# Splitting one chunk in five of the softmax probabilities on GpSimd, with GpSimd's weight work in the attention's written order

## The chip, the cores and the metric

The kernel runs on one core of one Trainium2 chip. The metric is the device time in microseconds (us) of one execution. The engines are TensorE (PE, whose weight loads have a row of their own, PEld), VectorE (DVE), ScalarE (ACT), GpSimd (POOL) and SyncE (SP), which issues every DMA of this kernel.

## What is computed

Two layers of a block with four mixers side by side, over 1024 latent rows and 256 context rows of width 1024. In each layer a conditioning vector gives scale, shift and gate (the modulation, `silu(c) @ w_mod`), the normalised rows go through one in-projection, two attention mixers (MLA and GQA, four heads each), a state-space scan and a long convolution run on slices of it, and an out-projection joins them. Cut to what matters here:

```python
def block_attention(q, k, v, scale):
    def attend(qblk):
        s = jnp.einsum('bqhgd,bkhd->bhgqk', qblk, k, preferred_element_type=jnp.float32) * scale
        p = jax.nn.softmax(s, axis=-1).astype(v.dtype)
        return jnp.einsum('bhgqk,bkhd->bqhgd', p, v)
...
for l in range(DEPTH):
    need_ctx = l < DEPTH - 1
    sh_l, sc_l, gt_l = [m[:, None, :] for m in modulation(c, w_mod[l], b_mod[l])]
    h_l = rms_norm(x, g_pre[l]) * (1 + sc_l) + sh_l
    p_l = h_l @ w_in[l]
    a_l, a_c = mla_mixer(...)
    g_l, g_c = gqa_mixer(...)
    out_l = jnp.concatenate([a_l, g_l, s_l, y_l], axis=-1) @ w_out[l]
    x = x + gt_l * rms_norm(out_l, g_post[l])
```

Latent queries attend to 1280 keys (1024 latent, 256 context), context queries to the 256 of the context. Context outputs are needed in layer 0 only.

## The kernel before, in words

**Products of two halves.** Most fp32 products are made of three fp32r products: an operand x is split into hi, a copy that rounds it to the type float32r, and lo = x - hi (`lo`, L248, a subtraction on VectorE unless another engine is named). An SBUF tile of halves is written `...h`/`...l` or `...hi`/`...lo`.

**Attention.** `attention` (L1528 on) runs once a layer: from 737 to 1077 us for layer 0 and from about 1820 to 2077 us for layer 1. A unit is one head and 256 queries. Layer 0 has 40 units (two GQA head pairs, then two MLA pairs; in each five blocks of 256 queries, the last of the context; two heads in each), layer 1 has 32. In a unit TensorE makes scores `aS` (latent keys) and `acx` (context keys), VectorE takes their maxima and scales (`am`), ScalarE makes the exponentials `aP` and their sums. The 1280 keys are five chunks of 256, c = 0 to 4. For each chunk TensorE transposes the probabilities into PSUM (`apt`, `tr` at L1651, step T of a chunk), ScalarE copies them to SBUF as float32r (`aPh`, `hi` at L1661, step H), VectorE subtracts (`aPl`, `lo` at L1665, step L), and TensorE multiplies both halves with the values (`apo`, `PV` at L1669, steps Vh and Vl). `apt` shares two PSUM banks (tag `f`) with the modulation products `mps` and the transposes `alb`; `aPh` and `aPl` have three buffers each. The softmax's denominators are summed and inverted on VectorE (`recip`, L1679), spread over 64 columns by GpSimd (`aLB`, `spread` at L1685), transposed (`alb`), and multiplied into the output (`aob`), which is stored.

**The order.** The program is written in the Tile framework; a scheduler places each engine's instructions by a simulated timeline (L1996), except for those that carry one issue-order token: these keep their written order on their engine. `keep` (L193) stamps the token that is set; inside `attention` it is set, and the written order is the table `ORDER` (L1525), which names the steps of a unit and, by +1 or -1, of which neighbouring unit. The DMA loads of keys, values and queries have a token of their own (`fetch`, L1548). The last entry, `X`, is `pump` (L1538), once a unit: it runs the products that the last pump left behind and draws one piece of side work, with the token taken off while it is drawn:

```python
            self.token = None
            more = next(side, self)
            self.token = token
```

**Side work.** `side` (L1934) first splits modulation weights: a piece (`mod_steps`, L325) takes one loaded block `mraw` of 128x1024, copies it to `mhi` and subtracts to `mlo`, both on GpSimd, and leaves four products `mps` and VectorE's addition to `msb` for the next pump. Layer 0 has 24 such pieces (its own gates and layer 1's modulation), layer 1 has 8 (its gates). The finished rows of the gates go out by a store `modg<-msb` (`mod_gates`, L375, the store at L381). Then the pool of these tiles is closed, a pool for the weights of the out-projection is opened in its place (L1941), and 16 pieces (`out_weights`, L1750) each take one loaded block `owr`, copy it to `owh` (L1757) and subtract to `owl`, again on GpSimd. Raw blocks are loaded two (`mraw`) or three (`owr`) pieces ahead by `feed` (L303).

Of the kernel before, what the change touches and what calls it, by code (L numbers as in the profile page):

```python
# [11 lines left out]
F32 = mybir.dt.float32  # L12
# [175 lines left out]
class K:  # L188
# [31 lines left out]
    def f(self, name="f"):  # L220
        return self.psf.tile([128, 512], F32, tag="f", name=name)
# [103 lines left out]
    def mod_steps(self, P, feed, l, blk):  # L325

        ms = P.tile([4, 512], F32, tag="msb", name="msb", bufs=2)
        nc = self.nc
        for k in range(0, 8, 2):
            raw = next(feed)  # L330
            hi, lo = (P.tile([128, 2, 512], F32R, tag="m" + t, name="m" + t, bufs=2) for t in ("hi", "lo"))
            nc.gpsimd.tensor_copy(hi, raw)
            self.lo(lo, raw, hi, nc.gpsimd)

            def products(k=k, hi=hi, lo=lo):
                ps = self.f("mps")
                for j in range(2):
                    self.mm(ps[:4], self.sp[:, k + j], hi[:, j], j == 0, False)
                    self.mm(ps[:2], self.sp[:, k + j, 0:2], lo[:, j], False, j == 1)
                if k == 0:  # L340
                    self.keep(nc.vector.tensor_copy(ms, ps[:4]))
                else:
                    self.tt(ms, ps[:4], ms, ADD)

            self.later.append(products)
            yield ms if k == 6 else None
# [1181 lines left out]
    def attention(self, l, pools, nq, side):  # L1528


        nc = self.nc

        W, L, P = pools
        token = self.token = f"att{l}"
# [3 lines left out]
        def pump():  # L1538

            late, self.later = self.later, []  # L1540
            for f in late:
                f()
            self.token = None
            more = next(side, self)
            self.token = token
            return more is not self or bool(self.later)

        def fetch(dst, src):  # L1548
# [102 lines left out]
        def tr(c, x):  # L1651
            ps = self.f("apt").rearrange("p (k q) -> p k q", k=2)
            for k in range(2):
                for qi in range(2):
                    j = 2 * c + k
                    self.tr(ps[:, k, qi * 128:qi * 128 + 128], x["pt"][qi][:, j * 128:j * 128 + 128])
            hi = W.tile([128, 2, 256], F32R, tag="aPh", name="aPh", bufs=3)
            lo = W.tile([128, 2, 256], F32R, tag="aPl", name="aPl", bufs=3)
            x["P"][c] = (ps, hi, lo)

        def hi(c, x):  # L1661
            ps, h, _ = x["P"][c]
            self.keep(nc.scalar.copy(h, ps))  # L1663

        def lo(c, x):  # L1665
            ps, h, l_ = x["P"][c]
            self.lo(l_, ps, h)

        def PV(c, part, x):  # L1669

# [50 lines left out]
        for c in range(5):  # L1721
            for nm, f in (("T", tr), ("H", hi), ("L", lo)):
                steps[f"{nm}{c}"] = partial(f, c)
            steps[f"Vh{c}"] = partial(PV, c, 1)
            steps[f"Vl{c}"] = partial(PV, c, 2)
        order = []
        for s in self.ORDER.split():
            if s == "X":
                order.append((pump, None, False))
                continue  # L1730
            nm, off = (s[:-2], int(s[-2:])) if s[-2:-1] in ("+", "-") else (s, 0)
            latent = nm[0] in "SM" and nm != "MC" or nm[0] in "THLV" and nm != "LB" and nm[-1] != "4"
            order.append((steps[nm], off, latent))
# [11 lines left out]
        while pump():  # L1745
            pass
# [3 lines left out]
    def out_weights(self, l, P, R):  # L1750
        wh = P.tile([128, 8, 1024], F32R, name="owh")
        wl = P.tile([128, 8, 1024], F32R, name="owl")
        halves = [(k, slice(h, h + 512)) for k in range(8) for h in (0, 512)]
        feed = self.feed(R, "owr", [128, 512], (self.A["w_out"][l, :, k, h] for k, h in halves), 3)
        for k, h in halves:
            raw = next(feed)
            self.nc.gpsimd.tensor_copy(wh[:, k, h], raw)  # L1757
            self.lo(wl[:, k, h], raw, wh[:, k, h], self.nc.gpsimd)
            yield
        self.wo = wh, wl  # L1760
# [239 lines left out]
```

## Time and profile before

| | |
|---|---|
| three runs | 2193.89, 2194.62, 2198.0 us; median 2194.62 |
| the profiled execution | 2194.1 us, span 2192.3 us |
| TensorE busy | 1937.6 us, 88% |
| VectorE busy | 1593.3 us, 73% |
| ScalarE busy | 916.5 us, 42% |
| GpSimd busy | 992.0 us, 45% |
| mean granted clock of TensorE | 0.927 of full |

The profile is of one execution, so its rows are compared with 2194.1 us; 1.8 us of that lie outside the span. Busy shares are means over stages that differ: a change in the attention is read from the attention's rows.

### The profile page before, as it was taken

How to read it: one execution, taken by the hardware profiler on the slowest of the kernel's cores; microseconds unless marked ns; L12 is line 12 of the kernel's file. 1: busy time of each engine (PE TensorE's matmuls, PEld its weight loads, DVE VectorE, ACT ScalarE, POOL GpSimd, SP SyncE). 2: the span in 40 equal slices, each digit the busy share in tenths (PEclk: the TensorE clock that was granted, in tenths of full speed). 3: DMA queues.
4: the chain of work that ended last, by engine and by line, in shares of the span. 5: the costliest groups of instructions: out<-in, count | busy, mean ns of one | idle time of the engine just before them, and what ended most of it. 6: DMA issues, size and time to landing. Idle time of an engine off the chain costs nothing.

```text
span 2192.3 us, 31534 instructions
## 1 busy us (share of the span) xinstructions
PE 1937.6 (88%) x10811; PEld 1617.4 (74%) x10811; DVE 1593.3 (73%) x2982; ACT 916.5 (42%) x1958; POOL 992.0 (45%) x798
## 2 busy tenths in 40 slices
PE   5788998789899899999799998997989949999888
PEld 2577887678778777788577776886767737899866
DVE  8799439855896589789444598389577858999732
ACT  4421233224334467667322322343233317788611
POOL 3757225564661244432155557246675622340034
PEclk7798899899999899999799987998999979999989
DMA  6323365337765546352343423264357673551053
GB/s 222 115 88 119 129 203 142 92 115 212 237 186 183 159 127 180 101 149 69 114 156 113 151 100 144 86 232 145 98 173 221 202 231 100 137 159 54 21 176 131
DMA packets 261249, 316.55 MB, mean 144 GB/s; under 512 B 46655, under 2 KB 203583, under 8 KB 257762
## 3 DMA queue, kind: packets, MB, share of 16 engines
q1 hardware_dynamic: 261090, 314.55, 47.0%
q8 instruction: 85, 1.39, 0.3%
q14 instruction: 74, 0.61, 0.1%
HBM read 207.61 MB, written 106.86 MB: 143 GB/s over the span
## 4 chain that ended last, share of the span: by engine, by line
PE 44%; DVE 29%; DMA 10%; issue 6%; POOL 5%; SPq 3%; ACT 2%; POOLq 0%; DVEq 0%; ACTq 0%
PE ipc L224 8%; PE apo L224 7%; PE ops L224 6%; PE aS L224 6%; PE apt L253 6%; DVE lU L233 3%; DVE sD L233 3%; SPq L201 3%; PE acx L224 2%; DVE sp L233 1%; PE mps L224 1%; DMA aq<-gP 1%; DVE aPl L233 1%; DVE lX L233 1%; PE fdft L224 1%
## 5 line engine op out<-in xcount | busy, mean ns | idle before, releaser
L224 PE MATMUL ipc<-hh,whi 128*128 128x512 f32 (+2 forms) x992 | 386.6, 390 | 18.8 <-DVE rs L512 6.9
L224 PE MATMUL ipc<-hl,whi 128*128 128x512 f32 (+2 forms) x992 | 380.9, 384 | 1.6 <-POOL hl L233 1.6
L224 PE MATMUL ipc<-hh,wlo 128*128 128x512 f32 (+2 forms) x992 | 379.8, 383 | 0.3 <-POOL wlo L233 0.3
L233 DVE TENSOR_TENSOR aPl<-apt,aPh 128x512 fp32r<-128x512 f32 x328 | 224.0, 684 | 20.9 <-ACT aPh L1663 17.0
L1663 ACT CAST aPh<-apt 128x512 fp32r<-128x512 f32 x328 | 186.5, 590 | 123.4 <-PE apt L253 115.4
L233 POOL TENSOR_TENSOR wlo<-wraw,whi 128x512 fp32r<-128x512 f32 x108 | 162.6, 1510 | 161.2 <-ACT whi L453 158.5
L224 PEld LDWEIGHTS ipc<-hh,whi 128*128 128x128 f32 x992 | 196.4, 198 | 51.9 <-DVE rs L512 7.9
L224 PEld LDWEIGHTS ipc<-hh,wlo 128*128 128x128 f32 x992 | 196.3, 198 | 30.9 <-issue 1.8
L224 PEld LDWEIGHTS ipc<-hl,whi 128*128 128x128 f32 x992 | 196.8, 198 | 29.9 <-POOL hl L233 2.3
L253 PE MATMUL apt<-ident,aP 128*128 128x128 f32 x1312 | 190.6, 276 | 1.0 <-DVE aPl L233 1.0
L224 PE MATMUL aS<-kst,aq 128*128 128x512 f32 x512 | 153.7, 423 | 20.5 <-DMA aq<-gP 14.9
L1628 DVE TENSOR_REDUCE am<-aS 128x1 f32<-128x1024 f32 x128 | 155.6, 1216 | 15.0 <-PE aS L224 15.0
L1691 POOL COPY aLB<-am 128x128 f32<-128x128 f32 x72 | 21.0, 291 | 313.6 <-DVE am L1683 313.6
L246 ACT ACTIVATE aP<-aS,am,rs 128x1024 f32<-128x1024 f32 x128 | 155.6, 1215 | 15.3 <-DVE am L243 14.2
L253 PEld LDWEIGHTS apt<-ident,aP 128*128 128x128 f32 x1312 | 149.1, 141 | 14.8 <-DVE aPl L233 6.4
L224 PE MATMUL apo<-aPh,vst 128*128 128x256 f32 x656 | 138.2, 308 | 14.9 <-ACT aPh L1663 9.0
L224 PE MATMUL apo<-aPl,vst 128*128 128x256 f32 x656 | 123.8, 286 | 3.0 <-DVE aPl L233 2.9
L224 PEld LDWEIGHTS apo<-aPh,vst 128*128 128x128 f32 x656 | 96.4, 190 | 29.9 <-DVE aob L233 14.8
L453 ACT CAST whi<-wraw 128x512 fp32r<-128x512 f32 x124 | 75.4, 618 | 101.9 <-PE ipc L224 56.6
L224 PEld LDWEIGHTS aS<-kst,aq 128*128 128x128 f32 x512 | 88.7, 194 | 35.5 <-issue 15.8
L224 PE MATMUL ops<-owh,omh 128*128 128x512 f32 x288 | 94.4, 408 | 19.4 <-ACT omh L1776 13.6
L224 PEld LDWEIGHTS apo<-aPl,vst 128*128 128x128 f32 x656 | 100.3, 190 | 10.0 <-DVE aPl L233 5.3
(368 smaller groups left out, 4485.7 us busy)
## 6 DMA issues: line engine op xcount, KB each, us to landing
wraw<-in_w_col_dram SPq DMA_DIRECT2D x64, 256.0 KB, 2.9
mraw<-in_w_mod_dram SPq DMA_DIRECT2D x32, 512.0 KB, 5.3
kst<-mK SPq DMA_DIRECT2D x16, 640.0 KB, 10.8
omx<-mixD SPq DMA_DIRECT2D x18, 512.0 KB
ogt<-gD SPq DMA_DIRECT2D x18, 512.0 KB, 4.6
wraw<-in_w_mod_dram SPq DMA_DIRECT2D x32, 256.0 KB, 4.0
k<-kt SPq DMA_DIRECT2D x16, 512.0 KB
lk<-k SPq DMA_DIRECT2D x8, 1024.0 KB, 6.1
```

The lines of the kernel that those rows point to most:

```text
L201: return self.nc.sync.dma_start(out=out, in_=in_)
L224: self.keep(self.nc.tensor.matmul(out, lhsT, rhs, start=start, stop=stop))
L233: self.keep((eng or self.nc.vector).tensor_tensor(out=out, in0=a, in1=b, op=op))
L246: self.keep(self.nc.scalar.activation(out=out, in_=in_, func=func, **k))
L253: self.keep(self.nc.tensor.transpose(out, in_, self.ident[:p, :p]))
L453: self.nc.scalar.copy(hi, raw)
L1628: self.keep(nc.vector.tensor_reduce(out=x["m"][:, 2 + qi:3 + qi], in_=x["S"][qi], axis=AX.X, op=ALU.max))
L1663: self.keep(nc.scalar.copy(h, ps))
L1691: self.keep(nc.gpsimd.tensor_copy(x["LB"][:, :, o:o + 64], x["m"][:, 10:12].unsqueeze(2).to_broadcast([128, 2, 64])))
```

## The change

In chunk 2 of each latent unit ScalarE's copy keeps fp32 and goes to a new SBUF tile `aPf` with two buffers; GpSimd makes `aPh` of it by a copy and `aPl` by a subtraction, where VectorE made `aPl` before. The other four chunks stay. Besides, GpSimd's pieces of side work get the token: the copies `mhi` and `owh` are kept, and `pump` no longer takes the token off, so all of GpSimd's work inside the attention follows the written order, the pump at a unit's end.

```diff
--- before.py
+++ after.py
@@ -329,7 +329,7 @@
         for k in range(0, 8, 2):
             raw = next(feed)
             hi, lo = (P.tile([128, 2, 512], F32R, tag="m" + t, name="m" + t, bufs=2) for t in ("hi", "lo"))
-            nc.gpsimd.tensor_copy(hi, raw)
+            self.keep(nc.gpsimd.tensor_copy(hi, raw))
             self.lo(lo, raw, hi, nc.gpsimd)
 
             def products(k=k, hi=hi, lo=lo):
@@ -1540,9 +1540,7 @@
             late, self.later = self.later, []
             for f in late:
                 f()
-            self.token = None
             more = next(side, self)
-            self.token = token
             return more is not self or bool(self.later)
 
         def fetch(dst, src):
@@ -1659,12 +1657,19 @@
             x["P"][c] = (ps, hi, lo)
 
         def hi(c, x):
-            ps, h, _ = x["P"][c]
-            self.keep(nc.scalar.copy(h, ps))
+            ps, h, l_ = x["P"][c]
+            if c == 2:
+
+                f = W.tile([128, 2, 256], F32, tag="aPf", name="aPf", bufs=2)
+                self.keep(nc.scalar.copy(f, ps))
+                self.keep(nc.gpsimd.tensor_copy(h, f))
+                x["P"][c] = (f, h, l_)
+            else:
+                self.keep(nc.scalar.copy(h, ps))
 
         def lo(c, x):
             ps, h, l_ = x["P"][c]
-            self.lo(l_, ps, h)
+            self.lo(l_, ps, h, nc.gpsimd if c == 2 else None)
 
         def PV(c, part, x):
 
@@ -1754,7 +1759,7 @@
         feed = self.feed(R, "owr", [128, 512], (self.A["w_out"][l, :, k, h] for k, h in halves), 3)
         for k, h in halves:
             raw = next(feed)
-            self.nc.gpsimd.tensor_copy(wh[:, k, h], raw)
+            self.keep(self.nc.gpsimd.tensor_copy(wh[:, k, h], raw))
             self.lo(wl[:, k, h], raw, wh[:, k, h], self.nc.gpsimd)
             yield
         self.wo = wh, wl
```

**GpSimd, layer 1, units 8 and 9.** Here the modulation weights end and those of the out-projection begin. Before, the first rows of out-projection work are four copies, and the spread `aLB` of a later unit stands ahead of the first subtraction:

```order
L1691 COPY aLB_17766<-am_17461 128x2x64 [waits DVE_49]
L1757 CAST owh_17803<-owr_17805 128x512
L1757 CAST owh_17803<-owr_17807 128x512 [waits DMAHW2_49]
L1757 CAST owh_17803<-owr_17809 128x512
L1757 CAST owh_17803<-owr_17811 128x512
L1691 COPY aLB_17999<-am_17579 128x2x64 [waits DVE_49,PE_49,Pool_49]
L233 TENSOR_TENSOR owl_17804<-owr_17805,owh_17803 128x512 [waits DMAHW5_49,PE_49,Pool_49]
L233 TENSOR_TENSOR owl_17804<-owr_17807,owh_17803 128x512 [waits Pool_49]
```

With the change the rows of units 8 and 9 are these (`aPf` is the new fp32 copy of the probabilities, `am` the denominators):

```order
L1665 CAST aPh_17818<-aPf_17827 128x512 [waits DVE_49,Activation_49]
L233 TENSOR_TENSOR aPl_17819<-aPf_17827,aPh_17818 128x512 [waits PE_49,Pool_49]
L1696 COPY aLB_17848<-am_17425 128x2x64 [waits DVE_49]
L1762 CAST owh_17885<-owr_17887 128x512 [waits DMAHW0_49]
L233 TENSOR_TENSOR owl_17886<-owr_17887,owh_17885 128x512 [waits DMAHW4_49,DMAHW5_49,DVE_49,Pool_49]
L1665 CAST aPh_17946<-aPf_17955 128x512 [waits Activation_49]
L233 TENSOR_TENSOR aPl_17947<-aPf_17955,aPh_17946 128x512 [waits PE_49,Pool_49]
L1696 COPY aLB_17848<-am_17537 128x2x64 [waits DVE_49]
L1762 CAST owh_17885<-owr_17889 128x512 [waits DMAHW1_49]
L233 TENSOR_TENSOR owl_17886<-owr_17889,owh_17885 128x512 [waits Pool_49]
```

Each unit now has copy, subtraction and spread, and one copy and one subtraction of weights behind them; the first `owl` stands between unit 8's spread and unit 9's copy `aPh`, and waits on DMA queues, VectorE and GpSimd.

**SyncE, the same place, with the change.** The store of the last gate rows stands behind four loads of keys (`kst`) and one of values (`vst`), as it does before the change:

```order
L201 DMA kst_18339<-mK1_15344 64x2560 [waits DMAHW0_49,Activation_49]
L201 DMA kst_18339<-mK1_15344 64x2560 [waits DMAHW1_49]
L201 DMA kst_18342<-mK1_15344 64x2560 [waits DMAHW2_49]
L201 DMA kst_18342<-mK1_15344 64x2560 [waits DMAHW3_49]
L201 DMA vst_18333<-mV1_15347 128x10x384 [waits DMAHW4_49]
L201 DMA modg1_16935<-msb_17410 4x512 [waits DMAHW5_49,DVE_49]
L201 DMA owr_18000<-in_w_out_dram 128x512 [waits DMAHW6_49,Pool_49]
L201 DMA owr_18111<-in_w_out_dram 128x512 [waits DMAHW7_49,Pool_49]
```

The two `owr` loads that follow it are those of later pieces of side work.

**VectorE, one unit of layer 1.** Before:

```order
L233 TENSOR_TENSOR aob_17767<-aob_17767,alb_17954 128x256 [waits DVE_49,PE_49]
L1628 TENSOR_REDUCE am_17687<-aS_17943 128x1
L243 TENSOR_SCALAR am_17687<-am_17687,nrs_15284 128x1 [waits DVE_49]
L233 TENSOR_TENSOR aPl_17972<-apt_17966,aPh_17971 128x512 [waits Activation_49]
L233 TENSOR_TENSOR am_17579<-am_17579 128x2
L1683 RECIPROCAL am_17579<-am_17579 128x2 [waits DVE_49]
L233 TENSOR_TENSOR aPl_17979<-apt_17973,aPh_17978 128x512 [waits Activation_49]
```

With the change, in the same place:

```order
L233 TENSOR_TENSOR aob_17849<-aob_17849,alb_18038 128x256 [waits DVE_49,PE_49]
L1626 TENSOR_REDUCE am_17767<-aS_18027 128x1
L243 TENSOR_SCALAR am_17767<-am_17767,nrs_15348 128x1 [waits DVE_49]
L233 TENSOR_TENSOR am_17657<-am_17657 128x2
L1688 RECIPROCAL am_17657<-am_17657 128x2 [waits DVE_49]
L233 TENSOR_TENSOR aPl_18063<-apt_18057,aPh_18062 128x512 [waits Activation_49]
L1626 TENSOR_REDUCE am_17900<-aS_18067 128x1 [waits PE_49]
```

The subtraction `aPl` between the scale (`nrs`) and the sum of the denominators (`am<-am`) is gone; what stands around it is the same.

## Rows read from the trace of the kernel before

**Rows 1.** Page, part 4: the chain that ended last, shares by engine

```profile
PE 44%; DVE 29%; DMA 10%; issue 6%; POOL 5%; SPq 3%; ACT 2%; POOLq 0%; DVEq 0%; ACTq 0%
```

**Rows 2.** Stretches, layer 1: length, busy (x) by engine, PEclk, DMA, GB/s

```profile
1846.88:1864.13 17.25, 17.00 (x116) 13.91 (x116) 15.86 (x29) 13.17 (x29) 7.45 (x6) 1.00 0.24 74
1922.25:1937.16 14.91, 14.91 (x106) 13.37 (x106) 14.60 (x28) 12.99 (x29) 9.11 (x11) 1.00 0.38 116
1977.60:1993.93 16.33, 16.33 (x120) 15.25 (x119) 15.23 (x27) 13.09 (x29) 0.59 (x2) 1.00 0.15 42
```

**Rows 3.** Groups by line, whole span: busy, mean ns | idle before, releasers

```profile
L233 DVE TENSOR_TENSOR aPl<-apt,aPh 128x512 fp32r<-128x512 f32 x328 | 224.0, 684 | 20.9 <-ACT aPh L1663 17.0
...
L233 POOL TENSOR_TENSOR wlo<-wraw,whi 128x512 fp32r<-128x512 f32 x108 | 162.6, 1510 | 161.2 <-ACT whi L453 158.5 <-PE ipc L224 2.3
...
L233 POOL TENSOR_TENSOR mlo<-mraw,mhi 128x1024 fp32r<-128x1024 f32 x32 | 76.2, 2385 | 1.9
...
L233 POOL TENSOR_TENSOR owl<-owr,owh 128x512 fp32r<-128x512 f32 x32 | 40.8, 1287 | 8.1 <-DMA modg<-msb 4.9 <-DVE scl L236 3.2
...
L332 POOL CAST mhi<-mraw 128x1024 fp32r<-128x1024 f32 x32 | 33.3, 1041 | 126.1 <-DMA mraw<-in_w_mod_dram 65.7 <-PE mps L224 53.9 <-issue 5.0
...
L1757 POOL CAST owh<-owr 128x512 fp32r<-128x512 f32 x32 | 19.2, 612 | 21.0 <-DMA owr<-in_w_out_dram 20.9
```

**Rows 4.** Waits, 746 to 1060, then 1846.88 to 1890: us, times, longest

```profile
DVE msb L233 <- PE mps L224: 11.1, 15, 1.3
PEld apo L224 <- DVE aob L233: 10.2, 18, 1.3
...
DVE msb L233 <- PE mps L224: 2.2, 4, 0.6
```

**Rows 5.** Timeline, layer 1, unit 9: start us, us, engine line op xcount

```profile
1897.25 1.08 ACT L1663 CAST aPh<-apt 128x512 fp32r<-128x512 f32 x2
1899.19 0.72 PE L224 MATMUL apo<-aPh,vst 128*128 128x256 f32 x4
1899.74 0.64 PE L224 MATMUL apo<-aPl,vst 128*128 128x256 f32 x4
```

**Rows 6.** Tile apt: duration ns min/median/max, first and last start

```profile
L233 DVE TENSOR_TENSOR aPl<-apt,aPh x328: 669/682/695, 747.8 to 2075.4; 128x512 fp32r<-128x512 f32 x164
```

**Rows 7.** Timeline, SyncE's queue, layer 1

```profile
1890.78 2.45 SPq L201 DMA_DIRECT2D kst<-mK  x4
1893.27 1.48 SPq L201 DMA_DIRECT2D vst<-mV  x1
1894.85 6.58 SPq L201 DMA_DIRECT2D modg<-msb  x1
```

**Rows 8.** Timeline, GpSimd, layer 1: in brackets idle time and releaser

```profile
1906.75 0.29 POOL L1691 COPY aLB<-am 128x128 f32<-128x128 f32 x1 [5.32 <-DVE am L1683]
1911.94 3.77 POOL L233 TENSOR_TENSOR owl<-owr,owh 128x512 fp32r<-128x512 f32 x3 [4.90 <-DMA modg<-msb]
```

**Rows 9.** Stretches around the first attention and near the end of the last

```profile
728.10:737.70 9.60, 2.32 (x21) 2.14 (x19) 1.11 (x2) 0.48 (x2) 0.00 (x0) 0.78 1.05 256
737.70:746.00 8.30, 7.23 (x20) 5.56 (x21) 4.11 (x6) 3.69 (x8) 1.61 (x2) 0.50 1.04 370
746.00:760.00 14.00, 14.00 (x98) 12.81 (x97) 13.51 (x25) 11.96 (x27) 5.75 (x5) 0.96 0.30 94
2089.00:2096.00 7.00, 4.96 (x12) 3.48 (x13) 1.91 (x5) 1.84 (x2) 2.36 (x1) 0.54 0.54 154
```

**Rows 10.** Timeline, GpSimd, layer 0

```profile
959.41 2.54 POOL L233 TENSOR_TENSOR owl<-owr,owh 128x512 fp32r<-128x512 f32 x2 [3.21 <-DVE scl L236]
964.35 0.29 POOL L1691 COPY aLB<-am 128x128 f32<-128x128 f32 x1 [2.40 <-DVE am L1683]
```

**Rows 11.** Stretch of layer 1 between the attentions, and TensorE's longest wait there

```profile
1240.00:1820.00 580.00, 496.01 (x2589) 414.78 (x2588) 439.53 (x843) 176.83 (x394) 308.01 (x220) 0.90 0.51 162
...
PE sglu L224 <- DVE sz L236: 18.1, 2, 12.7
```

## The prediction

> **What bounds the kernel now.** The two attention stretches run from 737 to 1077 us and from about 1820 to 2077 us; the change edits only them, so I read those first. The chain of waits says that the whole kernel hangs on TensorE before VectorE [rows 1]. The stretches table then takes three pairs of units of the second layer [rows 2]. In units that also carry modulation products (17.25 us for two) TensorE is busy 17.00 and VectorE 15.86. In plain units of the second attention kind, GQA (14.91 us for two), TensorE is busy all of it and VectorE 14.60. In MLA units (16.33 us for two) TensorE is busy all of it, VectorE 15.23. The reader is to see that VectorE is nearly full but that TensorE is at least as full. GpSimd is the free engine: 0.59 to 9.11 us of these stretches.
>
> **Part 1: VectorE loses one subtraction of five.** Of the 328 subtractions `aPl` at 684 ns [rows 3], chunk 2 has one in each of the 64 latent units (32 in each layer). That takes 64 x 0.684 = 43.8 us off VectorE; the piece of order in front shows it gone between a scale step (`nrs`) and the sum of the denominators. What of it is on the path? Three cases:
> - 32 MLA units: TensorE has no idle time there [rows 2]. Worth 0.
> - 24 GQA units with modulation products (16 in layer 0, 8 in layer 1): VectorE already arrives early and waits for TensorE's product `mps`, 11.1 us in layer 0 and 2.2 us in a stretch of layer 1, while TensorE waits 10.2 us for VectorE's `aob` [rows 4]. That is a ring: `mps`, then on VectorE `msb`, the context maximum, the scale, the first subtraction, `aob`, then TensorE again. Chunk 2 is not in it. What VectorE is given it waits for `mps`. Worth 0.
> - 8 plain GQA units of layer 1: VectorE is busy 14.60 of 14.91 us, but so is TensorE. At most 8 x 0.684 = 5.5 us; I take 1.5.
>
> The bounds of part 1 are 0 and a gain of 32 x 0.684 = 21.9 us (every GQA unit as short as VectorE's share allows; a busy TensorE is not one at its peak). I take **-1.5**, near the row that has TensorE full.
>
> **Part 2: GpSimd gets a copy and a subtraction per unit.** By the same shapes, `owh` and `owl`, these take 0.61 and 1.29 us [rows 3]. With the modulation split (1.04 and 2.39) that makes 5.3 us in a unit of 8.6, so the engine has room. ScalarE's copy only changes its type. Is GpSimd in time? In unit 9 of layer 1 ScalarE's two copies start at 1897.25 and take 1.08 together, so the first ends near 1897.79; GpSimd would then have the high half at 1898.40 and the low half at 1899.69. TensorE takes them at 1899.19 and, as the last two of four that start at 1899.74, near 1899.98 [rows 5]. That leaves 0.8 and 0.3 us: worth 0 while the queue ahead is empty, with up to 0.3 us a unit as the bad end (32 GQA units: +10).
>
> Does GpSimd slow VectorE? The subtraction takes 669 to 695 ns over all 328 [rows 6], with GpSimd at 0.59 or 9.11 us of a stretch, so 0. The Trainium skill, GPSIMD Engine Reference, Key points, says that GpSimd shares its SBUF interfaces with VectorE and contends with its instructions of two SBUF inputs. VectorE's subtraction here has one of its inputs in PSUM; by that rule the sum stays as it is.
>
> **Part 3: GpSimd's other work is now held in the written order.** Here is the expensive step. In layer 1 the modulation weights end with unit 7, and the weights of the out-projection begin at the end of unit 8. Their buffers lie where the modulation buffers were, so the first `owl` must wait until the last `modg<-msb` store has landed. That store is issued at 1894.85 behind four loads of keys and one of values, and SyncE spends 6.58 us on it [rows 7]; GpSimd's `owl` is released by it at 1911.94, 17 us after issue [rows 8]. Before, that wait cost nothing: GpSimd's spreads of the denominators slipped past it. Now the order in front puts copy and subtraction of unit 9, which TensorE needs, right **behind** that `owl`, and the store still stands behind the same five loads on SyncE.
>
> So: `owl` ends at 1911.94 + 1.29 = 1913.23; the copy of unit 9 at 1913.84; its subtraction at 1915.13. TensorE, in order, stops at the high half (slot 1899.19, 14.7 us late) and again at the low half (slot 1899.98): 1915.13 - 1899.98 = **15.2 us** lost. Behind the product in TensorE's queue are the next unit's scores, so VectorE and ScalarE starve too; nothing covers it. Low end: 0, if the store lands before it is needed; high end: the 15.2 and a little for the refill.
>
> The clock: after 9.60 us in which TensorE was busy only 2.32, the next 8.30 us were granted 0.50 (1.2 GHz) and then 0.96 of full; at 2089, after another gap, 7.00 us at 0.54 [rows 9]. So some 6.4 to 9.4 us of work at half speed follow a gap like this, and lose half of themselves: 3.2 to 4.7. I take **+3.5**, near the shorter, since not every microsecond there is TensorE's alone.
>
> In layer 0 the same seam waits for VectorE's `scl`, not for a store: `owl` started at 959.41 [rows 10], and its unit's next copy is due near 963 (the denominators of that unit are spread at 964.35). Worth 0. The other loads that GpSimd waits for are issued two or more units ahead on SyncE in the new order; 0.
>
> **Part 4: the middle of layer 1 is written in another order.** The scheduler moves scan products some 15 to 40 products earlier among those of the in-projection. TensorE is busy 496 of 580 us there, and its longest single wait is 12.7 us [rows 11]. One such wait more or less is the bound on either side; I take 0.
>
> **Sum.** The rows come from an execution of 2194.1 us (median of the runs 2194.62, 0.5 above). 2194.1 - 1.5 + 0 + 15.2 + 3.5 + 0 = 2211.3, say **2211 us**, 0.8% slower.
>
> **The rivals.**
> A. *The store is not late, so there is no stall* (not slower). The Trainium skill, DMA: Bandwidth & Descriptors, Queues, rings and completion order, says that completion is not first-in first-out per issuing engine, so that a small transfer may be complete before an earlier large one. By rows, the point that decides is landing before about 1896, when GpSimd would have to be through `owl` to copy at 1897.8; that is within 2 us of issue. Against it: 17 us in the trace [rows 7, 8], and the same five loads ahead. Then 2194.1 - 1.5 = 2192.6, within 0.2%, or, if VectorE's relief counts in part or in full, 2172 to 2189. Chance 0.18: 0.08 for no change and 0.10 for faster.
> B. *GpSimd late in every GQA unit* on top of the stall. The margin is 0.3 us, and the same subtraction, as `wlo`, takes 1510 ns on the kernel's mean [rows 3], 0.22 more. 32 x 0.3 = +10: 2221 us. For it: the margin is thin. Against: attention's own `owl` is the shorter. Chance 0.08.
> C. *The stall is there, and VectorE's relief pays* 4 to 12 us more than I say: 2199 to 2207. For it: VectorE at 14.60 of 14.91. Against: TensorE at all of it. Chance 0.08.
>
> **How the numbers follow.** The forecast has 0.66 and spans 2203 to 2218 through clock, refill and the reordered middle. A measurement of this kernel tells 0.2% (4.4 us) from no change. Slower by more: 0.66 + 0.08 + 0.08 = 0.82; within 0.2%: 0.08; faster: 0.10. The range 2199 to 2221 takes in B and C and leaves out A (0.18) and little else.
>
> **What would show it.** In the changed profile GpSimd should have one idle stretch of 15 us or more before the first `owl` of layer 1, ended by the store `modg<-msb`; TensorE should stand idle for 12 to 15 us in the same place, ended by GpSimd's copy, with the granted clock at half behind it. VectorE should show 264 subtractions `aPl` (328 - 64), with its idle time before `msb` up by about half a microsecond a unit, and the pairs of units within 0.5 us of 17.25, 14.91 and 16.33. I am wrong if that idle stretch is short, or if the unit pairs shrink by 1 us or more, or if TensorE waits for GpSimd's halves in many units.

## The result and the profile after

The changed kernel takes 2213.03 us (median of 4 runs, 2210.53 to 2218.15) where the kernel before takes 2196.31 (4 runs): a ratio of 1.0081, 95% interval 1.0063 to 1.0098. It is slower by 0.8%. The forecast was 2211, the range 2199 to 2221. The profiled execution took 2214.21 us, its span is 2212.4, 20.1 more than the span before.

Cut at VectorE's reciprocals of the denominators (one a unit, their starts read from the trace), the two profiled executions differ in these places:

| stretch, us | before | after | difference |
|---|---|---|---|
| start to the first unit of layer 0 | 751.3 | 749.7 | -1.6 |
| attention of layer 0 | 311.8 | 311.1 | -0.7 |
| between the attentions | 759.4 | 764.8 | +5.4 |
| layer 1, units 0 to 8 | 68.0 | 67.7 | -0.3 |
| units 8 to 10 | 16.0 | 32.5 | **+16.5** |
| units 10 to 16 | 47.0 | 46.0 | -1.0 |
| units 16 to 31 | 120.1 | 119.5 | -0.6 |
| last unit to the end | 118.8 | 121.1 | +2.2 |

The place forecast holds most of it. First the chain of work that ended last, within units 8 to 10 of layer 1 (start, us, what; `issue` is time in which the engine waited for nothing that the profile shows):

```profile
1897.39 0.37 DVE am L1623
1897.76 16.85 DMA modg<-msb
...
1914.77 0.04 POOL owl L233
1914.81 1.16 issue
1915.97 0.62 POOL aPh L1665
1916.60 0.04 issue
1916.64 2.15 PE apo L224 x8
```

The chain runs through the store of a few gate rows, then GpSimd's first `owl`, then the high half of unit 9, then TensorE's products. GpSimd's and SyncE's timelines there (start, us, operation; in brackets the idle time and its releaser) are the counterparts of [rows 7, 8]:

```profile
1894.84 0.62 POOL L1762 CAST owh<-owr 128x512 fp32r<-128x512 f32 x1
1914.77 1.26 POOL L233 TENSOR_TENSOR owl<-owr,owh 128x512 fp32r<-128x512 f32 x1 [19.31 <-DMA modg<-msb]
1915.97 0.61 POOL L1665 CAST aPh<-aPf 128x512 fp32r<-128x512 f32 x1
1916.67 1.28 POOL L233 TENSOR_TENSOR aPl<-aPf,aPh 128x512 fp32r<-128x512 f32 x1
```

```profile
1894.35 2.67 SPq L201 DMA_DIRECT2D kst<-mK  x4
1897.06 0.60 SPq L201 DMA_DIRECT2D vst<-mV  x1
1897.76 6.91 SPq L201 DMA_DIRECT2D modg<-msb  x1
```

The store lands 16.9 us after its issue began, as before. Next come TensorE's longest waits in layer 1's attention (columns as in [rows 4]), and the stretches of the stall, of what follows it, and of full speed again (columns as in [rows 2], the engines in the order PE, PEld, DVE, ACT, POOL):

```profile
PEld apo L224 <- POOL aPh L1665: 14.2, 1, 14.2
PE apo L224 <- POOL aPh L1665: 13.9, 1, 13.9
```

```profile
1902.72:1916.64 13.92, 0.00 (x0) 0.00 (x1) 1.38 (x2) 1.05 (x4) 1.82 (x2) 0.58 0.81 219
1916.64:1922.60 5.96, 5.96 (x27) 5.88 (x28) 2.08 (x4) 1.28 (x3) 3.34 (x4) 0.55 0.30 88
1922.60:1930.00 7.40, 7.40 (x56) 6.86 (x55) 6.87 (x13) 6.50 (x15) 3.99 (x5) 1.00 0.31 91
```

TensorE does nothing for 13.92 us, then works 5.96 us at a granted clock of 0.55, then at full. At 0.55, 0.45 x 5.96 = 2.7 us are lost: 13.9 + 2.7 = 16.6, the 16.5 of the table.

The pairs of units away from that place, in the order of [rows 2]:

```profile
1850.22:1867.40 17.18, 16.92 (x117) 13.90 (x116) 15.37 (x28) 13.31 (x29) 11.02 (x10) 1.00 0.29 85
1940.64:1955.52 14.88, 14.88 (x108) 13.43 (x107) 13.69 (x26) 13.13 (x29) 7.97 (x10) 1.00 0.30 80
1995.63:2011.96 16.33, 16.33 (x120) 15.24 (x119) 14.25 (x25) 13.29 (x29) 7.96 (x11) 1.00 0.34 95
```

VectorE is 0.5 to 1.0 us a pair less busy and the pairs are as long as they were: TensorE fills them. The subtractions by group (columns as in [rows 3]):

```profile
L233 DVE TENSOR_TENSOR aPl<-apt,aPh 128x512 fp32r<-128x512 f32 x264 | 181.0, 686 | 60.0 <-ACT aPh L1668 57.9
...
L233 POOL TENSOR_TENSOR aPl<-aPf,aPh 128x512 fp32r<-128x512 f32 x64 | 82.6, 1291 | 5.1
L233 POOL TENSOR_TENSOR owl<-owr,owh 128x512 fp32r<-128x512 f32 x32 | 41.1, 1285 | 26.0 <-DMA modg<-msb 19.3 <-DVE scl L236 4.3
L1665 POOL CAST aPh<-aPf 128x512 fp32r<-128x512 f32 x64 | 39.4, 616 | 332.8 <-ACT aPf L1664 199.9 <-DVE am L1626 64.2 <-DVE am L243 54.3
```

VectorE lost 224.0 - 181.0 = 43.0 us of subtractions and its idle time ahead of the other 264 rose from 20.9 to 60.0, by 39.1: what it was given it waits, for ScalarE's copies.

### The profile page after: what moved, and what is told of

Same layout as the page of the kernel before. It is cut to its first block, busy times and chain, and to the rows that moved or that the text cites. A ratio compares the mean times of both kernels' runs of the same rounds, so it can differ in the third digit from the quotient of the medians.

```text
span 2212.4 us, 31552 instructions
## 1 busy us (share of the span) xinstructions
PE 1944.6 (88%) x10811; PEld 1621.2 (73%) x10811; DVE 1555.3 (70%) x2918; ACT 920.7 (42%) x1958; POOL 1109.8 (50%) x926
## 4 chain that ended last, share of the span: by engine, by line
PE 47%; DVE 27%; DMA 9%; issue 7%; POOL 4%; SPq 3%; ACT 2%; POOLq 0%; DVEq 0%; ACTq 0%
PE ipc L224 10%; PE apo L224 7%; PE aS L224 6%; PE ops L224 6%; PE apt L253 6%; SPq L201 3%; DVE sD L233 2%; DVE lU L233 2%; PE acx L224 2%; DVE sp L233 1%; PE mps L224 1%; DVE lX L233 1%; PE lout L224 1%; DMA omx<-mixD 1%; DVE pww L233 1%
## 5 line engine op out<-in xcount | busy, mean ns | idle before, releaser
L233 POOL TENSOR_TENSOR wlo<-wraw,whi 128x512 fp32r<-128x512 f32 x108 | 157.4, 1462 | 159.0 <-ACT whi L453 142.2
L233 DVE TENSOR_TENSOR aPl<-apt,aPh 128x512 fp32r<-128x512 f32 x264 | 181.0, 686 | 60.0 <-ACT aPh L1668 57.9
L1668 ACT CAST aPh<-apt 128x512 fp32r<-128x512 f32 x264 | 155.6, 591 | 125.7 <-PE apt L253 105.0
L1665 POOL CAST aPh<-aPf 128x512 fp32r<-128x512 f32 x64 | 39.4, 616 | 332.8 <-ACT aPf L1664 199.9
L224 PE MATMUL apo<-aPh,vst 128*128 128x256 f32 x656 | 138.7, 309 | 27.8 <-POOL aPh L1665 13.9
L253 PEld LDWEIGHTS apt<-ident,aP 128*128 128x128 f32 x1312 | 150.0, 141 | 12.7 <-DVE aPl L233 6.5
L224 PEld LDWEIGHTS apo<-aPl,vst 128*128 128x128 f32 x656 | 102.0, 190 | 10.7 <-DVE aPl L233 4.1
```

The lines of the kernel that those rows point to most:

```text
L224: self.keep(self.nc.tensor.matmul(out, lhsT, rhs, start=start, stop=stop))
L233: self.keep((eng or self.nc.vector).tensor_tensor(out=out, in0=a, in1=b, op=op))
L253: self.keep(self.nc.tensor.transpose(out, in_, self.ident[:p, :p]))
L1665: self.keep(nc.gpsimd.tensor_copy(h, f))
```

## The experiments

Theory W says that the loss is the wait of the first `owl` for the store, with unit 9's halves queued behind it. Rival G says that GpSimd's halves are late or slow by themselves; rival M, that the other written order between the attentions is most of it. Times are medians; every ratio is to the kernel before, run beside it on the same chip. Lengths of stretches are cut as in the table above.

**1. `msb` in a place of its own** (`msb_own`), in the changed kernel:

```diff
-        ms = P.tile([4, 512], F32, tag="msb", name="msb", bufs=2)
+        ms = self.mp.tile([4, 512], F32, tag="msb", name="msb", bufs=2)
...
+            k.mp = R
             with k.pool("ma", side="right") as M:
```

> The rows of the modulation result `msb` get a place that the out-projection's weights do not reuse, so the first `owl` of layer 1 no longer waits for the store; the order of TensorE, VectorE and ScalarE is that of the changed kernel. Theory W (the wait in GpSimd's queue is the loss): GpSimd's 19.3 us and TensorE's 13.9 us of waiting in units 8 to 10 go, the clock stays at full there, units 8 to 10 take about 16 us where they took 32.5; 2195 to 2199 us, since the 5.4 us between the two attentions and the 2.2 us of the tail stay. Rival G (GpSimd's halves of chunk 2 are late or slow by themselves): units 8 to 10 stay above 28 us, time at 2208 or more. Rival M (the other written order between the attentions is most of it): at 2210 or more.

Measured: 2198.68 us, ratio 1.0007 (0.9994 to 1.0021), 14 us under the changed kernel. The first `owl` waits 1.34 us, units 8 to 10 are back at full clock and at 16.00 us:

```profile
1895.30 1.29 POOL L233 TENSOR_TENSOR owl<-owr,owh 128x512 fp32r<-128x512 f32 x1 [1.34 <-PE mps L224]
```

```profile
1891.80:1907.80 16.00, 15.78 (x112) 13.68 (x111) 14.71 (x27) 13.34 (x29) 7.97 (x10) 1.00 0.94 222
```

G and M fall: chunk 2 is still on GpSimd, TensorE's written order is still the changed one, and the time is that of before.

**2. The first weights of the out-projection drawn four units later** (`delay`), in the changed kernel:

```diff
+            for _ in range(4 * l):
+                yield
             O = wo.enter_context(k.pool("wo", side="right"))
```

> As the changed kernel, but in layer 1 the first piece of out-projection weights is drawn four units later, by when the store has landed (12 units of 32 then have no side work or none left). W: the first `owl` waits less than 1 us; the same 2195 to 2199 us as with `msb` in its own place, and 1 us less or more for the tail. G: 2208 or more.

Measured: 2200.99 us, ratio 1.0018 (1.0007 to 1.0030), 1 us above what was expected even with the 1 us for the tail. Units 8 to 10 take 16.0 us. The first `owl` starts as soon as its copy is done:

```profile
1929.94 0.61 POOL L1762 CAST owh<-owr 128x512 fp32r<-128x512 f32 x1
1930.63 1.28 POOL L233 TENSOR_TENSOR owl<-owr,owh 128x512 fp32r<-128x512 f32 x1
```

**3. The written order alone** (`order_only`): the kernel before with the two `keep` and without the two lines on the token in `pump`; chunk 2 stays on VectorE.

> The kernel before with GpSimd's side work in the written order, chunk 2 left on VectorE. W: the first `owl` now stands ahead of unit 9's spread, which TensorE needs at 1903.0 (its transposes `alb`) and which then ends at about 1913.5: a wait of 10.5 us and some 3 us of half clock, 2194 + 13.5 = 2205 to 2210 us, give or take the order between the attentions. G: with nothing of chunk 2 on GpSimd, within 4 us of 2194.

Measured: 2192.56 us, ratio 0.9980 (0.9969 to 0.9990): faster, where I expected 2205 to 2210. The time alone is what rival G gave, within 4 us of 2194; the trace tells them apart. The stall is there and ends at the spread, TensorE's wait as sized (10.7 us for 10.5):

```profile
POOL owl L233 <- DMA modg<-msb: 20.9, 1, 20.9
PEld alb L253 <- POOL aLB L1689: 11.1, 1, 11.1
PE alb L253 <- POOL aLB L1689: 10.7, 1, 10.7
```

Units 8 to 10 take 27.4 us, +11.4 for the 13.5 expected with the clock. What I had not reckoned with lies elsewhere: the stretch between the attentions, where the program text is untouched, fell from 759.4 to 745.6 us. Here it is in the kernel before, the changed one and this one (three traces, columns as in [rows 2]):

```profile
1063.10:1822.50 759.40, 655.85 (x3262) 538.24 (x3262) 510.95 (x968) 227.32 (x481) 399.73 (x285) 0.90 0.50 157
```

```profile
1060.90:1825.70 764.80, 658.27 (x3259) 539.38 (x3260) 511.89 (x967) 226.82 (x481) 394.94 (x284) 0.90 0.49 154
```

```profile
1064.10:1809.70 745.60, 655.14 (x3260) 538.50 (x3261) 514.80 (x968) 226.63 (x481) 390.10 (x283) 0.91 0.51 158
```

TensorE's work is the same to 3 us; its idle time is 103.6, 106.5 and 90.5 us. The scheduler wrote TensorE's products there in another order in each of the three.

**4. Chunk 2 alone** (`chunk_only`): the changed kernel with the token taken off the side work again, as before.

> The changed kernel with the token taken off the side work again, chunk 2 on GpSimd. The scheduler puts the first `owl` behind unit 9 and ahead of unit 10's copy, and three more `owl` ahead of unit 10's subtraction. W: the subtraction ends at about 1911.9 + 1.3 + 0.6 + 3.9 + 1.3 = 1919.0 where TensorE wants it at 1907.6; 11.4 us of wait and 3 of clock: 2206 to 2211 us, give or take the order between the attentions. A theory that the written order of the side work is what costs: 2192 to 2196. G: about 2213, spread over all units.

Measured: 2234.75 us, ratio 1.0167 (1.0147 to 1.0187). Right in sign, far off in size: the attention of layer 0 takes 333.3 us (+21.5), units 10 to 16 of layer 1 take 73.9 (+26.9), and 13.5 come back between the attentions. TensorE's waits for GpSimd in layer 0, and GpSimd's timeline at one place there:

```profile
PE apo L224 <- POOL aPl L233: 16.9, 6, 5.9
```

```profile
826.96 4.72 POOL L233 TENSOR_TENSOR mlo<-mraw,mhi 128x1024 fp32r<-128x1024 f32 x2
```

and in layer 1:

```profile
PE apo L224 <- POOL aPl L233: 13.2, 4, 7.7
...
POOL owl L233 <- DMA modg<-msb: 10.5, 1, 10.5
...
PE apo L224 <- POOL aPh L1667: 7.6, 1, 7.6
```

```profile
1929.86 3.71 POOL L233 TENSOR_TENSOR owl<-owr,owh 128x512 fp32r<-128x512 f32 x3
1933.54 1.26 POOL L233 TENSOR_TENSOR aPl<-aPf,aPh 128x512 fp32r<-128x512 f32 x1
```

Left free, the scheduler puts two `mlo` or several `owl` in a row, and attention's halves stand behind them. I had looked only at the seam of layer 1. So the chunk needs the written order; the written order does not need the chunk.

**5 and 6. The written order and `msb` in its own place, without the chunk** (`order_msb`: edits 1 and 3 on the kernel before) **and with it in layer 1 alone** (`l1_chunk_msb`: edit 1 on the changed kernel, and `c == 2 and l == 1`). TensorE's written order is that of experiment 3 in both.

> Chunk 2 on VectorE, GpSimd's side work in the written order, `msb` in a place of its own; TensorE's written order is that of the run with the order alone. W: units 8 to 10 at 16 us where that run took 27.4, the 745.6 us between the attentions kept: 2192.6 - 11.4 = 2181 us (2178 to 2184). If the 13.7 us between the attentions were chance of one profile: about 2194.

> The same, with chunk 2 on GpSimd in layer 1 alone; TensorE's written order is again the same. TensorE bounds the units (as the prediction has it): 1 to 3 us less than the run without the chunk, in the units 10 to 16 (46 for 47) and after (119.5 for 120.1). VectorE bounds them: up to 32 x 0.684 = 22 us less. GpSimd late: more than the run without.

Measured: 2180.44 us, ratio 0.9939 (0.9921 to 0.9956), without the chunk; 2182.87, ratio 0.9948 (0.9927 to 0.9969), with it. Units 8 to 10 take 16.0 in both, the stretch between the attentions 743.2 and 746.4. With the chunk I had expected 1 to 3 us less than without; it took 2.4 more, the two intervals overlap, and so no gain of the chunk shows.

**7. The subtraction left out** (`no_sub`, edit 1 on the changed kernel): chunk 2 has one copy, on ScalarE, and its low product takes the high half.

```diff
             if c == 2:
 
-                f = W.tile([128, 2, 256], F32, tag="aPf", name="aPf", bufs=2)
-                self.keep(nc.scalar.copy(f, ps))
-                self.keep(nc.gpsimd.tensor_copy(h, f))
-                x["P"][c] = (f, h, l_)
+                self.keep(nc.scalar.copy(h, ps))
+                x["P"][c] = (ps, h, h)
...
-            self.lo(l_, ps, h, nc.gpsimd if c == 2 else None)
+            if c != 2:
+                self.lo(l_, ps, h)
```

> With `msb` in its own place and side work in the written order, chunk 2's subtraction is left out altogether: its low product takes the high half instead (the output is not the reference's). It is VectorE's relief with no work on GpSimd. TensorE bounds: attention of layer 0 at 309 to 312 us, of layer 1 at 248 to 251 from the first reciprocal to the last (251.0 before). VectorE bounds: 22 us less in each layer.

Measured: 2185.29 us in one run; the attention of layer 0 takes 309.7 us. The attention of layer 1 from the first reciprocal to the last, without the chunk on GpSimd, with it, and with the subtraction gone altogether (three traces):

```profile
1809.50:2059.90 250.40, 248.08 (x1756) 221.78 (x1754) 233.11 (x423) 201.14 (x430) 65.73 (x79) 1.00 0.37 102
```

```profile
1811.30:2061.20 249.90, 247.70 (x1754) 221.76 (x1752) 219.63 (x391) 203.80 (x430) 122.67 (x141) 1.00 0.38 103
```

```profile
1814.10:2063.60 249.50, 247.30 (x1752) 221.46 (x1750) 218.20 (x390) 201.10 (x430) 65.68 (x79) 1.00 0.38 102
```

VectorE is busy 233.11, 219.63 and 218.20 us and the length moves by 0.9 at most. TensorE is busy all but 2.2 to 2.3 us in each. This settles part 1: the attention does not get shorter when VectorE has less to do.

**8. The store from ScalarE's queue** (`store_act`), in the changed kernel: `nc.scalar.dma_start` in place of `self.store` in `mod_gates`.

> The changed kernel with the gates' store issued from ScalarE's queue in place of SyncE's; TensorE's written order the same. Q (it is late because it stands behind five loads in SyncE's queue): it lands within some 4 us of its issue, the first `owl` starts before 1906 and units 8 to 10 take 18 to 26 us. D (it is late because those loads keep the transfer engines full): the `owl` starts at 1912 or later as before, units 8 to 10 take 30 us or more.

Measured: 2209.69 us in one run, units 8 to 10 at 23.7 us. ScalarE's queue and GpSimd (two timelines):

```profile
1901.94 0.25 ACTq L1542 DMA_DIRECT2D modg<-msb  x1
```

```profile
1910.77 1.26 POOL L233 TENSOR_TENSOR owl<-owr,owh 128x512 fp32r<-128x512 f32 x1 [10.78 <-DMA modg<-msb]
```

The store lands 8.7 us after its issue, not 17, and not within the 4 of Q; neither Q nor D holds as it was put. The queue explains half of the delay; with the store in another queue the rest stays. From 1902 to 1910.8, the store's issue to its landing, the DMA column stands at 0.99: the transfer engines are busy with the loads.

**9. The store ahead of the loads on SyncE** (`store_first`), in the changed kernel: the store of `mod_gates` gets the loads' token `ald{l}`.

> The changed kernel with the gates' store held in the written order of the loads of keys, values and queries, so that SyncE issues it ahead of the four loads of keys and the one of values; everything else as in the changed kernel, TensorE's written order the same. W, with the store late because of those five loads: it lands within about 3 us of its issue, `owl` waits less than 2 us for it, units 8 to 10 take 16 to 18 us, time 2196 to 2201 us as with `msb` in its own place. If the store is late for another reason (VectorE's last `msb`, a slow store of four rows): units 8 to 10 stay at 24 us or more, 2205 or more.

Measured: 2203.99 us, ratio 1.0036 (1.0021 to 1.0051). SyncE issues the store in 0.28 us and the `owl` is released by VectorE, 1.6 us later:

```profile
1901.36 0.28 SPq L201 DMA_DIRECT2D modg<-msb  x1
...
1906.87 3.07 SPq L201 DMA_DIRECT2D kst<-mK  x4
1909.98 0.60 SPq L201 DMA_DIRECT2D vst<-mV  x1
1910.68 7.69 SPq L201 DMA_DIRECT2D aq<-mQ  x1
```

```profile
1902.98 1.29 POOL L233 TENSOR_TENSOR owl<-owr,owh 128x512 fp32r<-128x512 f32 x1 [3.56 <-DVE aPl L233]
```

Units 8 to 10 take 16.0 us: the five loads ahead were what made the store late. The time is 3 us above what was expected, since the first store of the layer, issued at 1861.15, now holds back the loads of the next GQA pair behind it: those of the keys are issued at 1861.48, with `msb` in its own place at 1822.77. One of units 0 to 8 takes 14.3 us where it takes 8.4 there (units 0 to 8: 73.5 for 67.7).

## Why the prediction was right

The place, the chain and the releaser are those forecast, and that is not luck. That the sum meets the time within 2 us is in part luck: the forecast adds 17.2 us to the profiled execution, 18.7 of them at the stall. The two profiled executions differ there by 16.5 and by 3.6 in all the rest, with 5.4 between the attentions, where 0 was taken.

- **Part 3, the stall: right.** Place, chain and releaser are those forecast: 19.3 us of GpSimd, 13.9 of TensorE, for 15.2. Experiments 1, 2 and 9 remove it in three ways and get 14, 12 and 9 us of the 17 back (medians against the changed kernel's); each leaves chunk 2 on GpSimd.
- **The clock: right in kind, a little too large.** 2.7 us for the 3.5 taken, and under the 3.2 to 4.7 that I had given: 5.96 us at 0.55 after the gap, a little under the shorter of the two stretches I had [rows 9].
- **Part 1: right in its reason, the term too large.** -1.5 was taken. Chunk 2 on GpSimd in layer 1 is worth 250.4 - 249.9 = 0.5 us there, and 2182.87 stands against 2180.44 in all, intervals overlapping; layer 0 takes 310.3 to 311.2 us with it in written order (the changed kernel, experiments 1, 2, 8 and 9) and 309.6 to 310.8 without (3, 5 and 6): nothing. I had expected VectorE's freed time ahead of `msb`; that wait fell (8.9 us in layer 0 for 11.1), and the time appears ahead of the other subtractions.
- **Part 2: right.** Away from the seam no wait of TensorE for GpSimd's halves shows, and `aPh` and `aPl` take 616 and 1291 ns for the 612 and 1287 reckoned. VectorE's subtraction takes 686 ns for 684 with GpSimd at 8 to 11 us of a pair.
- **Part 4: the size was off.** 0 was taken. The order that the changed kernel shares with experiments 1, 2, 8 and 9 gives 764.8, 759.6, 762.7, 763.7 and 761.3 us between the attentions, a mean of 762.4 against the one 759.4 of before: +3, with 5.2 between the five themselves, so that the +3 is hardly clear of noise. The order of experiments 3, 5 and 6 gives 745.6, 743.2 and 746.4, and two further orders, of experiments 4 and 7, give 745.9 and 748.5. So such an order can be worth 14 us; the one wait of 12.7 that I took as the bound was none. What in the order costs or saves the time was not tried.
- **What is left** is -1.6 us ahead of the attention and +2.2 in the tail. Stretches of the same program text differ by as much between the runs here (749.7 to 757.9 us ahead of the attention); the tail is 118.8 to 119.8 us without chunk 2 on GpSimd in layer 1 and 120.1 to 121.3 with it on. About 0.6 of that is the last reciprocal coming earlier, the rest was not tried.

Rival A needed the store to land within 2 us. It does so in experiment 9 alone, where it is issued ahead of the loads. The Trainium skill, DMA: Bandwidth & Descriptors, Queues, rings and completion order, has it that completion is not first-in first-out per issuing engine. The trace of before agrees, but by too little to help: by the marks that finished transfers leave in it, the store was complete at 1911.78 and the load of values issued ahead of it at 1914.24. In the changed kernel the two were complete at 1914.61 and 1914.65, in both 17 us after the store's issue.

The best version is that of experiment 5, 2180.44 us, 0.6% under the kernel before: the written order for GpSimd's side work, no chunk on GpSimd, and `msb` where no weight reuses its place. Its gain comes from the stretch between the attentions (743.2 us for 759.4), which the scheduler happened to write better, and only to some 3 us from the attention.

## What to carry to other kernels

An engine's queue in written order makes every wait in it a wait for all that stands behind: before work on the critical path joins a queue, look for the latest releaser of what is already in it, a store of 8 KB behind five loads here. Here the relief of an engine that was 0.98 busy at most was worth no more than 0.9 us in a whole attention, while another was at 1.00; leaving the work out altogether is a cheap way to see that. Where a scheduler orders the rest of the program, compare that rest too: here it moved by 14 us on an edit far from it, enough to hide an 11 us stall.

## What the runs showed that was not expected

The same store took 16.9 us to land behind five loads on SyncE's queue, 8.7 from ScalarE's queue beside them, and 1.4 ahead of them. By their marks in the changed kernel the four loads of keys were complete at 1900.68, 1903.65, 1906.61 and 1909.71, the values at 1914.65 and the store at 1914.61: from SyncE's queue it came with the last of them. From ScalarE's queue (experiment 8) it was complete at 1910.60, ahead of three of the five, which were complete at 1912.40, 1915.71 and 1920.76. SyncE spent 6.91 us on issuing the store behind the loads and 0.28 ahead of them; in experiment 9 the load of queries that then stands behind the five takes 7.69, so this time goes with the place in the queue. And the stretch between the attentions took 743 to 765 us with TensorE busy for 651 to 661 of it: the runs of one written order lie within 3 to 5 us of each other, the means of the orders up to 17 apart.
